# A two-layer diffusion backbone: more work of the expert layers put between the decoding of the keys and its transposes

## The chip, the core and the metric

The kernel runs on one core of one Trainium2 chip. The metric is the device time of one execution in microseconds (us). The engines are TensorE (PE, matmuls), VectorE (DVE), ScalarE (ACT), GpSimd (POOL) and SyncE (SP, which here only starts DMAs). Each engine works through its own queue of instructions in order and waits at semaphores for the others.

## The reference, cut to what matters

A sequence of 256 latent tokens and 256 context tokens, 1024 wide, passes two layers. Each layer is a token mixer (layer 1: mLSTM, layer 2: RWKV-7) and a retrieval of experts (PEER). Six modulation rows per layer come from a product of a conditioning vector with `ada_w`. All is float32. The retrieval is where the change lies:

```
# 8 heads, 2 x 128 product keys, 16 picks per head, 128 x 128 = 16384 experts
q        = h @ wq                         # per head two halves of 128
s1, s2   = top16(q1 @ keys1), top16(q2 @ keys2)
gate, (i, j) = top16 of the sums s1 + s2  # softmax over 16; expert number = 128*i + j
y[t]     = sum over the 8*16 picks of  gate * gelu(h[t] . u[128*i + j]) * v[128*i + j]
```

The kernel does not gather per token. It computes gelu(h . u) for all 128 x 128 experts, "row" j of 128 experts at a time, multiplies by a gate matrix that is zero where an expert wasn't picked, and sums with all rows of `v`. Only 128 of the tokens in layer 1 go by gathers (`urows`, `vtab`) of their picked experts.

## The kernel before, in words

**Products.** A float32 product is three matmuls in a rounded format: a weight block is loaded raw (512 KB), ACT writes its high half (`hi_w`, L77), DVE or GpSimd the remainder (`lo_w`, L78: raw minus high), and `mm3` (L97 to L99) issues high by high, high by low, low by high. A row of `u` takes 24 such matmuls. In layer 1 (`peer_two`) a row is 384 columns wide (256 of the context, 128 latent tokens), its two lo halves are 512 wide each and raw data lies in a ring of seven slots called `unit`; in layer 2 (`peer_one`) a row is 256 columns wide, its lo half is one instruction 1024 wide, and rows go in pairs with one Gelu each (L1788). Both have three buffers for hi and for lo.

**Retrieval.** `retrieval` (L1253) computes queries and scores, takes the top 16, and decodes the picked pairs on DVE: a long run of small integer operations (L1344 to L1359) and four times a one-hot compare (L1364, 128 x 2048), a multiply (L1366), two sums (L1368) and a reduction (L1369) into `sel`. Then it calls `between`, in which a layer puts products of other rows, and behind that transposes the decoded keys `sel` (L1380) and the gates (L1385) on PE into `iT`, `jT` and `gT`, from which the gate matrices are built (one-hot matrices `A` on ACT, L1647 and L1648, `B` on DVE, products `gp`, L1672).

**Layer 1 around the change.** Rows 0 to 7 come first, for the context's columns only. `between` adds rows 8 to 19 with lo halves on GpSimd. After the transposes `u_rest` computes rows 20 to 51 (long) and then the missing columns of rows 0 to 7 (short, 128 wide), into slots A and C; beside it the 128 gathers go (L1580 on GpSimd, their dot products L1588 on DVE, `rows1` from L1566 holds the expert numbers). Every fourth row also advances `fill`, one modulation pass (`ada_pass`, L131: 16 loads of 512 KB into buffers of its own, 32 matmuls of 32 x 512, four transposes). Then the gate stage begins.

**Layer 2 around the change.** Rows 0 to 7, retrieval with rows 8 to 19 in `between` (lo halves on GpSimd), then rows 20 to 63 (odd rows and those below 24 on GpSimd, the rest on DVE), then the gates.

**Order.** The program is written through a tile framework whose scheduler sets the order of the instructions in each engine's queue by its own estimates; the order of the code is only its input. PSUM has eight banks; in layer 1 `u` rows rotate through b6 and b0, scores and transposes through b7 and b1, the modulation pass has b2, and b3 to b5 are not in use yet.

Of the kernel before, what the change touches and what calls it, by code (L numbers as in the profile page):

```python
# [12 lines left out]
F32 = DT.float32  # L13
# [23 lines left out]
def mkpool(tc, name, bufs=1, space=None, side=None):  # L37
    kw = dict(name=name, bufs=bufs, reuse_waits="tile")
    if space is not None:
        kw["space"] = space  # L40
    if side is not None:
        kw["side"] = side
    return tc.tile_pool(**kw)
# [38 lines left out]
def load_raw(E, src, n=1024, pool=None, bufs=None):  # L82
    raw = (pool or E.W).tile([128, n], F32, name="raw", tag="raw", bufs=bufs or E.rawbufs)
    if len(src.shape) == 3:
        E.nc.sync.dma_start(raw.rearrange("p (a b) -> p a b", a=src.shape[1]), src)
    else:
        E.nc.sync.dma_start(raw, src)
    return raw


def stream(E, src, n=1024, eng=None):
    return split(E, load_raw(E, src, n), E.W, "w", E.partbufs, n, eng)
# [35 lines left out]
    nc.scalar.activation(E.sc[:, :, 0:2].rearrange("p k s -> p s k"), cr, AF.Silu)  # L128


def ada_pass(E, A, l, q, mods, pool, ps_pool, tag, bufs, own=0, halves=(0, 1)):  # L131


    nc = E.nc
    ada_w, ada_b, mods_dr, modsT = A["ada_w"][l], A["ada_b"][l], E.mods_dr[l], mods[q]
    ps = ps_pool.tile([128, 512], F32, name="ada_ps", tag=tag, bufs=bufs)
    bt = pool.tile([128, 512], F32, name="ada_bt", bufs=1)
    nc.gpsimd.memset(bt, 0.0)
    offs = [q * 2048 + half * 1024 + n * 512 for half in halves for n in range(2)]
    for g, o in enumerate(offs):  # L140
        nc.sync.dma_start(bt[32 * g:32 * g + 2, :], rows_bc(ada_b[o:o + 512], 2))
    fetch = lambda kt: [load_raw(E, ada_w[kt * 128:(kt + 1) * 128, offs[2 * x]:offs[2 * x] + 1024], 1024,
                                 pool if own else None, own) for x in range(len(halves))]
    raws = fetch(0)
    for kt in range(KT):
        if kt:
            yield

        for g in range(len(offs)):
            nc.tensor.matmul(ps[32 * g:32 * g + 32, :], E.sc[:, kt, :], raws[g // 2][:, g % 2 * 512:g % 2 * 512 + 512],  # L150
                             start=kt == 0, stop=kt == KT - 1, tile_position=(0, 32 * g))
        if kt < KT - 1:
            raws = fetch(kt + 1)
    rows = slice(0, 32 * len(offs))
    nc.vector.tensor_tensor(bt[rows], ps[rows], bt[rows], op=ALU.add)
    for g, o in enumerate(offs):
        if o // D in (2, 5):
            nc.sync.dma_start(mods_dr[:, o:o + 512], bt[32 * g:32 * g + 2, :])
    cols = [x for x, half in enumerate(halves) if 2 * q + half != 5]
    if cols:  # L160
        tp = ps_pool.tile([128, 4, 4, 32], F32, name="ada_tp", tag=tag, bufs=bufs)
        for blk in range(4):
            nc.tensor.transpose(tp[:, blk].rearrange("p g s -> p (g s)"), bt[:, blk * 128:(blk + 1) * 128], E.ident)
        for s in range(2):
            for x in cols:
                nc.vector.tensor_copy(modsT[:, s, halves[x]].rearrange("p (g b) -> p g b", g=2),
                                      tp[:, :, 2 * x:2 * x + 2, s].rearrange("p b g -> p g b"))
        m = {0: 1, 2: 0}.get(q)
        if m in halves:
            nc.vector.tensor_scalar(modsT[:, :, m, :], modsT[:, :, m, :], 1.0, None, op0=ALU.add)  # L170
    yield
# [7 lines left out]
def advance(gen, n):  # L179

    for _ in gen:
        if n is not None:
            n -= 1
            if n <= 0:
                break
# [1250 lines left out]
def peer_two(E, H0, h1, end, wq, keysT, uT, urows, vtab, filler):  # L1436
# [23 lines left out]
    with open_w(E, 2, 3), ExitStack() as pc:  # L1460
# [70 lines left out]
        def u_rows(j0, j1, t0=0, eng=None):  # L1531
            for j in range(j0, j1):
                up = ps_u.tile([128, TD], F32, name="u_ps")
                u_prod(up[:, t0:], halves(load(uT[j]), eng), t0)
                S.activation(row(j)[:, t0:], up[:, t0:], AF.Gelu)  # L1535
                yield


        with mkpool(tc, "route", 1) as R:
            for j in range(0, EARLY, 2):  # L1540
                up = (ps_u, ps_m)[j // 2 % 2].tile([128, 2, T], F32, name="u0_ps")
                for x in range(2):
                    u_prod(up[:, x], halves(load(uT[j + x])), 0, T, H0)
                S.activation(slots[0][:, j:j + 2, 0:T], up, AF.Gelu)
            for x in range(2):
                for y in range(2):
                    S.activation(H[x][:, 4 * y:4 * y + 4, 0:T], H0[x][:, 4 * y:4 * y + 4].bitcast(F32), AF.Copy)
            turn[:] = 0, NU
            H1 = [R.tile([128, KT, T], F32R, name=f"hr{x}") for x in range(2)]
            for x in range(2):  # L1550
                raw = R.tile([128, 4, T], F32, name="hraw", tag="eq", bufs=1)
                nc.sync.dma_start(raw.rearrange("p k t -> p (k t)"), h1[x])
                ks = slice(4 * x, 4 * x + 4)
                S.activation(H1[0][:, ks], raw, AF.Copy)
                V.tensor_tensor(H1[1][:, ks], raw, H1[0][:, ks].bitcast(F32), op=ALU.subtract)
                for y in range(2):
                    S.activation(H[y][:, ks, T:], H1[y][:, ks, 0:128].bitcast(F32), AF.Copy)
                xp = ps_m.tile([128, 4, 128], F32, name="x_ps")
                for k in range(4):
                    nc.tensor.transpose(xp[:, k, :], raw[:, k, 128:T], E.ident)  # L1560
                S.activation(xt[:, x * 512:(x + 1) * 512], xp.rearrange("p k d -> p (k d)"), AF.Copy)

            def between(picked):
                gate, sel = picked[1]
                V.tensor_copy(gate1, gate[:, 1].rearrange("p h c -> p (h c)"))
                V.scalar_tensor_tensor(rows1, sel[:, 1, 1].rearrange("p h c -> p (h c)"), 128.0,  # L1566
                                       sel[:, 0, 1].rearrange("p h c -> p (h c)"), op0=ALU.mult, op1=ALU.add)
                advance(u_rows(EARLY, EARLY + LATER, eng=G), None)

            Hs = [[[t[:, kt, 0:T] for kt in range(KT)] for t in X] for X in (H, H1)]  # L1570
            retrieval(E, R, ps_u, ps_m, Hs, [(*i, g[:, :, 0], g[:, :, 1]) for i, g in zip(idx, gT)], wq, keysT,
                      between, load)
# [27 lines left out]
        def interleave(*gens):  # L1600

            todo = [[0.0, 1.0 / n, g] for g, n in gens]
            while todo:
                todo.sort(key=lambda t: t[0])
                t = todo[0]
                t[0] += t[1]
                try:
                    next(t[2])
                except StopIteration:
                    todo.remove(t)  # L1610
# [3 lines left out]
        def fetch(n):  # L1614
            return itertools.islice(fs, n), n
# [3 lines left out]
                          i[0].rearrange("p (g x t) -> p g x t", x=2, t=8)[:, :, 0])  # L1619
        PC = pc.enter_context(mkpool(tc, "slotC", 1))  # L1620
        slots.append(PC.tile([128, NA - NX, TD], F32, name="slotC"))
        with mkpool(tc, "early", 1) as X:
            fill = filler(X, ps, "b2", 1)

            def u_rest():
                for x, _ in enumerate(itertools.chain(u_rows(EARLY + LATER, NA), u_rows(0, EARLY, T))):
                    if x % 4 == 0:
                        advance(fill, 1)
                    yield

            interleave((u_rest(), NA - LATER), fetch(GS[0]))
            advance(fill, None)
        bctx = pc.enter_context(ExitStack())
        PB = bctx.enter_context(mkpool(tc, "slotB", 1))
        slots.append(PB.tile([128, NB, TD], F32, name="slotB"))
# [114 lines left out]
def peer_one(E, end, H0, wq, keysT, uT, vtab):  # L1750
# [6 lines left out]
    JH = 64  # L1757
    JP = 96
    EARLY = 8
    LATER = 12  # L1760
    with open_w(E, 3, 3), ExitStack() as pc:
        misc = pc.enter_context(mkpool(tc, "pmisc", 1))
        oh = pc.enter_context(mkpool(tc, "poh", 2))
# [14 lines left out]
        def u_pair(j, gated, early=False):  # L1778
            ps = ps_u.tile([128, 2, T], F32, name="u_ps", tag="u")
            for x in range(2):  # L1780
                proj(E, ps[:, x, :], stream(E, uT[j + x], eng=G if early and (x or j < 24) else None), H)
            sl = slot(j, 2)
            if gated:
                a = misc.tile([128, 2, T], F32, name="act", bufs=2)
                S.activation(a, ps, AF.Gelu)
                V.tensor_tensor(sl, sl, a, op=ALU.mult)
            else:
                S.activation(sl, ps, AF.Gelu)  # L1788
# [135 lines left out]
def build(tc, A, out):  # L1924
    with ExitStack() as ctx:
# [32 lines left out]
        def end1(u, ep, ps, tag, acc, y1=None):  # L1958
            s = 1 - u
            if u == 0:  # L1960
# [3 lines left out]
                                  m1[0][:, s, 1, :], h_tile=hk[u], bufs=2, y1=y1)  # L1964

        peer_two(E, H0, h1, end1, A["wqT"][0], A["keysT"][0], A["uT"][0], A["urows"], A["vtab"][0],
                 lambda *p: ada_pass(E, A, 1, 0, m1, *p, own=2))
        H3 = []

        def epi2(acc, ps, tag):  # L1970
# [96 lines left out]
```

## Time and profile before

| | us |
|---|---|
| runs of the kernel before | 3315.76, 3321.59, 3330.23 (median 3321.59) |
| the profiled execution, on the device | 3324.07 |
| its span in the profile | 3322.2 |
| PE busy | 3062.8 (92%) |
| DVE busy | 2472.1 (74%) |
| ACT busy | 1543.7 (46%) |
| GpSimd busy | 743.5 (22%) |

The profiled execution's own time is 1.9 us above its span, and 2.5 us above the median of the runs. Busy times overlap, so they say little of what the end waits for. The rows further down are taken from views of the trace: a timeline row has the start and the duration of an instruction (or of several equal ones in a row, x4), its engine, line and operation, and in brackets how long the engine had stood idle before it and what ended that; a row of grouped lines has the count, the busy time and the mean in ns; a row of windows has the busy time of PE, PE's weight loads, DVE, ACT and GpSimd in a stretch of 20 us, the granted clock of PE as a share of full speed, the share of the DMA engines that was busy, and GB/s.

### The profile page before, as it was taken

The page shows a single profiled execution, that of the slowest core. Times are in us where ns is not written, and L with a number is a line of the kernel's source. Part 1 is how long each engine was busy: PE and PEld are TensorE (multiplying, and loading weights), DVE is VectorE, ACT ScalarE, POOL GpSimd, SP SyncE. Part 2 cuts the span into 40 slices and gives each one's busy share as a digit, 9 for nine tenths or more (in the row PEclk, how much of TensorE's full clock was granted, in tenths as well). Part 3 has the DMA queues.
Part 4 walks back from the last instruction along what each step waited for, and adds up shares of the span by engine and source line. Part 5 has one row for each costly group of instructions (what it writes and reads, how often), then busy time and mean ns, then how long its engine had stood idle before and what let it go on. Part 6 is the DMA issues. An engine that isn't in the chain of part 4 may idle for free.

```text
span 3322.2 us, 54675 instructions
## 1 busy us (share of the span) xinstructions
PE 3062.8 (92%) x20325; PEld 2627.3 (79%) x20325; DVE 2472.1 (74%) x5438; ACT 1543.7 (46%) x2867; POOL 743.5 (22%) x660
## 2 busy tenths in 40 slices
PE   7999999899999899999997887778889799999998
PEld 4776799799988789877875764477878799888887
DVE  5838679757978788899788638995767529887555
ACT  3524343335733333465444447466744343444443
POOL 1010044331033333303342310021307430000000
PEclk8999999898999999999998999889999899999999
DMA  5236532585368788836884257675744454556554
GB/s 211 88 98 201 198 137 70 211 301 200 120 224 272 246 275 285 291 130 241 288 280 141 91 167 214 190 203 161 230 150 147 139 185 153 170 172 223 191 190 146
DMA packets 251882, 633.82 MB, mean 191 GB/s; under 512 B 39840, under 2 KB 97312, under 8 KB 251360
## 3 DMA queue, kind: packets, MB, share of 16 engines
q1 hardware_dynamic: 180672, 478.27, 43.8%
q0 software_dynamic: 37152, 135.28, 12.1%
q10 hardware_dynamic: 33792, 16.78, 1.8%
q8 instruction: 159, 2.61, 0.3%
q14 instruction: 107, 0.88, 0.1%
HBM read 589.06 MB, written 41.19 MB: 190 GB/s over the span
## 4 chain that ended last, share of the span: by engine, by line
PE 68%; DVE 17%; DMA 6%; issue 5%; ACT 2%; POOL 2%; SPq 0%; ACTq 0%; DVEq 0%; POOLq 0%
PE acc L1714 11%; PE acc L1819 11%; PE u_ps L97 8%; PE u_ps L99 7%; PE u_ps L98 7%; DMA unit<-urows,rows 2%; PE gp L1672 2%; PE ada_ps L150 2%; DVE lo_w L78 1%; DMA raw<-ada_w 1%; PE vo L99 1%; DVE o_qk L326 1%; PE vo L98 1%; PE vo L97 1%; DVE xm L666 1%
## 5 line engine op out<-in xcount | busy, mean ns | idle before, releaser
L77 ACT ACTIVATE hi_w<-raw 128x1024 fp32r<-128x1024 f32 x339 | 358.2, 1057 | 528.6 <-PE u_ps L98 228.8
L78 DVE TENSOR_TENSOR lo_w<-raw,hi_w 128x1024 fp32r<-128x1024 f32 x287 | 354.1, 1234 | 320.6 <-ACT hi_w L77 320.4
L77 ACT ACTIVATE hi_w<-unit 128x512 fp32r<-128x512 f32 x522 | 326.4, 629 | 494.1 <-PE u_ps L98 279.7
L78 DVE TENSOR_TENSOR lo_w<-unit,hi_w 128x512 fp32r<-128x512 f32 x498 | 337.9, 687 | 152.1 <-ACT hi_w L77 150.1
L99 PE MATMUL u_ps<-hd,lo_w 128*128 128x384 f32 (+1 forms) x1024 | 348.7, 341 | 24.4 <-DVE lo_w L78 20.8
L97 PE MATMUL u_ps<-hd,hi_w 128*128 128x384 f32 (+1 forms) x1024 | 352.3, 344 | 4.1 <-ACT hi_w L77 3.0
L98 PE MATMUL u_ps<-hd,hi_w 128*128 128x384 f32 (+1 forms) x1024 | 347.8, 340 | 0.0
L97 PE MATMUL u_ps<-carry,hi_w 128*128 128x256 f32 x1088 | 310.2, 285 | 4.5 <-ACT carry L210 4.5
L99 PE MATMUL u_ps<-carry,lo_w 128*128 128x256 f32 x1088 | 308.4, 283 | 5.9 <-POOL lo_w L78 5.9
L98 PE MATMUL u_ps<-carry,hi_w 128*128 128x256 f32 x1088 | 307.9, 283 | 0.0
L1714 PE MATMUL acc<-hi_w,wh 128*128 128x512 f32 x718 | 282.9, 400 | 7.9 <-ACT hi_w L77 6.2
L1714 PE MATMUL acc<-lo_w,wh 128*128 128x512 f32 x718 | 283.9, 395 | 5.5 <-DVE lo_w L78 5.4
L1714 PE MATMUL acc<-hi_w,wl 128*128 128x512 f32 x718 | 282.6, 394 | 0.0
L1580 POOL DMA_INDIRECT unit<-urows,rows x128 | 165.9, 1296 | 428.7 <-DVE unit L1588 249.7
L1580 POOL DMA_INDIRECT unit<-vtab,rows x128 | 179.9, 1406 | 360.9 <-DVE xt L1593 171.0
L99 PEld LDWEIGHTS u_ps<-hd,lo_w 128*128 128x128 f32 x1024 | 198.6, 194 | 29.3 <-DVE lo_w L78 24.3
L99 PEld LDWEIGHTS u_ps<-carry,lo_w 128*128 128x128 f32 x1088 | 207.3, 191 | 6.7 <-POOL lo_w L78 6.7
L97 PEld LDWEIGHTS u_ps<-carry,hi_w 128*128 128x128 f32 x1088 | 207.9, 191 | 5.5 <-ACT carry L210 4.9
L97 PEld LDWEIGHTS u_ps<-hd,hi_w 128*128 128x128 f32 x1024 | 198.8, 194 | 12.7 <-ACT slotC L1535 5.9
L98 PEld LDWEIGHTS u_ps<-carry,hi_w 128*128 128x128 f32 x1088 | 207.6, 191 | 0.8 <-DVE carry L211 0.2
L98 PEld LDWEIGHTS u_ps<-hd,hi_w 128*128 128x128 f32 x1024 | 198.5, 194 | 1.2
L1588 DVE SCALAR_TENSOR_TENSOR unit<-unit,xt 128x1024 f32<-128x1024 f32 x128 | 155.3, 1219 | 41.4 <-DMA unit<-urows,rows 41.4
(523 smaller groups left out, 7493.9 us busy)
## 6 DMA issues: line engine op xcount, KB each, us to landing
raw<-vtab SPq DMA_DIRECT2D x144, 512.0 KB
unit<-uT SPq DMA_DIRECT2D x136, 512.0 KB
unit<-vtab SPq DMA_DIRECT2D x128, 512.0 KB
raw<-uT SPq DMA_DIRECT2D x128, 512.0 KB
raw<-ada_w SPq DMA_DIRECT2D x96, 512.0 KB
PK<-dr_pk SPq DMA_DIRECT2D x64, 448.0 KB
raw<-w_qkT SPq DMA_DIRECT2D x16, 512.0 KB
raw<-w_in SPq DMA_DIRECT2D x16, 512.0 KB
```

Of the source, the lines that this page charges most:

```text
L77: nc.scalar.activation(hi, raw, AF.Copy)
L78: (eng or nc.vector).tensor_tensor(lo, raw, hi.bitcast(F32), op=ALU.subtract)
L97: mm(out, lhi, rhi, start=start, stop=False)
L98: mm(out, lhi, rlo, start=False, stop=False)
L99: mm(out, llo, rhi, start=False, stop=stop)
L150: nc.tensor.matmul(ps[32 * g:32 * g + 32, :], E.sc[:, kt, :], raws[g // 2][:, g % 2 * 512:g % 2 * 512 + 512], start=kt == 0, stop=kt == KT ...
L326: V.scalar_tensor_tensor(dst, src, cw[:, ct, k:k + 1], dst, op0=ALU.mult, op1=ALU.add)
L1580: G.indirect_dma_start(out=t, out_offset=None, in_=src, in_offset=bass.IndirectOffsetOnAxis(ap=rows1[:, s:s + 1], axis=0))
L1588: return V.scalar_tensor_tensor(t, t, 1.0, xt, op0=ALU.mult, op1=ALU.mult, accum_out=act[:, s:s + 1])
L1672: mm(gp[:, t], At[t], Bg[:, x, t // 2, :, t % 2], start=x == 0, stop=x == 1)
L1714: mm(accs[2 * tt + n], l[:, ts], r, start=j == 0 and y == 0, stop=j == 127 and y == 2)
L1819: mm(acc[tt * 2 + n], l[:, x, ts], r[:, n * 512:(n + 1) * 512], start=(j + x == 0 and l is wh and r is vhi), stop=(j + x == 127 and l is wl))
```

## The change

In layer 1 the modulation pass leaves `u_rest` and is issued whole inside `between`, with raw data in the ring of `unit` slots and not in buffers of its own. After it the products of rows 20, 21 and 22 go to the banks b3 to b5, lo halves on GpSimd; their Gelus follow once slot C is open. `u_rest` then holds 29 long and 8 short rows and no modulation pass. In layer 2 `LATER` goes from 12 to 28, so that rows 8 to 35 stand in `between`, all of them with lo halves on GpSimd.

```
-def ada_pass(E, A, l, q, mods, pool, ps_pool, tag, bufs, own=0, halves=(0, 1)):
+def ada_pass(E, A, l, q, mods, pool, ps_pool, tag, bufs, own=0, halves=(0, 1), load=None):
...
-    fetch = lambda kt: [load_raw(E, ada_w[kt * 128:(kt + 1) * 128, offs[2 * x]:offs[2 * x] + 1024], 1024,
-                                 pool if own else None, own) for x in range(len(halves))]
+    load = load or (lambda src: load_raw(E, src, 1024, pool if own else None, own))
+    fetch = lambda kt: [load(ada_w[kt * 128:(kt + 1) * 128, offs[2 * x]:offs[2 * x] + 1024])
+                        for x in range(len(halves))]
...
+            beside = []
+
             def between(picked):
...
                 advance(u_rows(EARLY, EARLY + LATER, eng=G), None)
+                advance(filler(R, ps, "b2", 1, load=load), None)
+
+                for x in range(3):
+                    beside.append((EARLY + LATER + x, ps.tile([128, TD], F32, name="u_ps", tag=f"b{3 + x}", bufs=1)))
+                    u_prod(beside[x][1], halves(load(uT[beside[x][0]]), G))
...
-        with mkpool(tc, "early", 1) as X:
-            fill = filler(X, ps, "b2", 1)
-
-            def u_rest():
-                for x, _ in enumerate(itertools.chain(u_rows(EARLY + LATER, NA), u_rows(0, EARLY, T))):
-                    if x % 4 == 0:
-                        advance(fill, 1)
-                    yield
-
-            interleave((u_rest(), NA - LATER), fetch(GS[0]))
-            advance(fill, None)
+        for j, up in beside:
+            S.activation(row(j), up, AF.Gelu)
+        u_rest = itertools.chain(u_rows(EARLY + LATER + len(beside), NA), u_rows(0, EARLY, T))
+        interleave((u_rest, NA - LATER - len(beside)), fetch(GS[0]))
...
 def peer_one
-    LATER = 12
+    LATER = 28
...
-                proj(E, ps[:, x, :], stream(E, uT[j + x], eng=G if early and (x or j < 24) else None), H)
+                proj(E, ps[:, x, :], stream(E, uT[j + x], eng=G if early and (x or j < EARLY + LATER) else None), H)
...
-                 lambda *p: ada_pass(E, A, 1, 0, m1, *p, own=2))
+                 lambda *p, **k: ada_pass(E, A, 1, 0, m1, *p, **k))
```

The lines of the changed kernel have numbers one higher than before from L139 on, and eight higher behind `between` of layer 1.

What the scheduler makes of it on PE in layer 1, at the transposes of the decoded keys. In the kernel before, the matmuls of row 20 (`u_ps`) go on between the transposes (`tp`), the first three of them ahead of the transposes of the gates:

```order
L99 MATMUL u_ps<-hd_3189,lo_w 128x384
L1380 MATMUL tp<-ident,sel 128x128 x4
L97 MATMUL u_ps<-hd_3189,hi_w 128x384
L98 MATMUL u_ps<-hd_3190,hi_w 128x384
L99 MATMUL u_ps<-hd_3189,lo_w 128x384
L1385 MATMUL tp<-ident,gate 128x128 x2
L97 MATMUL u_ps<-hd_3189,hi_w 128x384
L1380 MATMUL tp<-ident,sel 128x128
```

In the changed kernel the same place on PE reads (`ada_ps` is the modulation pass):

```order
L99 MATMUL u_ps<-hd_3189,lo_w 128x384
L151 MATMUL ada_ps<-unit,sc_lhs 32x512 x14
L1381 MATMUL tp<-ident,sel 128x128 x4
L151 MATMUL ada_ps<-unit,sc_lhs 32x512 x2
L1386 MATMUL tp<-ident,gate 128x128 x2
L1381 MATMUL tp<-ident,sel 128x128 x2
L1386 MATMUL tp<-ident,gate 128x128
L151 MATMUL ada_ps<-unit,sc_lhs 32x512 x4
L1673 LDWEIGHTS A
L1673 MATMUL gp<-Bg,A 128x52
```

The last two rows are the first of 16 such pairs (the first gate products); two ada matmuls, 16 more pairs, ten ada matmuls and the four transposes of the modulation pass follow, and only then the first matmul of row 20. So 14 of the 32 ada matmuls moved ahead of the transposes, and rows 20 to 22 did not.

On ACT in the changed kernel the same place has two complete builds of `A` ahead of all but one of the high halves of rows 20 to 22:

```order
L77 ACTIVATE hi_w<-unit 128x512
L1536 ACTIVATE slotA<-u_ps 128x384 x2
L1648 ACTIVATE A<-iota_65,iF_3182 128x128 x8
L1649 ACTIVATE A<-A 128x1024
L1648 ACTIVATE A<-iota_65,iF_3182 128x128 x8
L1649 ACTIVATE A<-A 128x1024
L77 ACTIVATE hi_w<-unit 128x512 x5
L1631 ACTIVATE slotC<-u_ps 128x384
```

Before, there was one build at this place, with high halves between its parts.

In layer 2, on PE, the place of the transposes in the kernel before:

```order
L98 MATMUL u_ps<-carry_24518,hi_w 128x256
L99 MATMUL u_ps<-carry_24517,lo_w 128x256
L1380 MATMUL tp<-ident,sel 128x128 x4
L97 MATMUL u_ps<-carry_24517,hi_w 128x256
L98 MATMUL u_ps<-carry_24518,hi_w 128x256
L99 MATMUL u_ps<-carry_24517,lo_w 128x256
L1385 MATMUL tp<-ident,gate 128x128 x2
```

The changed kernel has the same rows around its transposes, with 384 more matmuls (16 rows) ahead of them. On GpSimd the last run of lo halves goes from

```order
L1298 TENSOR_TENSOR cand<-sv 128x2x16
L78 TENSOR_TENSOR lo_w<-raw,hi_w 128x1024 x32
```

before to this in the changed kernel:

```order
L1299 TENSOR_TENSOR cand<-sv 128x2x16
L78 TENSOR_TENSOR lo_w<-raw,hi_w 128x1024 x38
```

The six more are the even rows 24 to 34, which DVE made before.

## Rows read from the trace of the kernel before

**Rows 1.** The page, the chain that ended last: its engines.

```profile
PE 68%; DVE 17%; DMA 6%; issue 5%; ACT 2%; POOL 2%; SPq 0%; ACTq 0%; DVEq 0%; POOLq 0%
```

**Rows 2.** Timeline of PE, layer 1, at the transposes.

```profile
594.59 0.34 PE L99 MATMUL u_ps<-hd,lo_w 128*128 128x384 f32 x1
594.77 0.60 PE L1380 MATMUL tp<-ident,sel 128*128 128x128 f32 x4
...
610.02 0.69 PE L99 MATMUL u_ps<-hd,lo_w 128*128 128x384 f32 x1 [14.30 <-DVE lo_w L78]
...
613.28 0.67 PE L97 MATMUL u_ps<-hd,hi_w 128*128 128x384 f32 x1
...
618.23 0.40 PE L98 MATMUL u_ps<-hd,hi_w 128*128 128x384 f32 x1
```

**Rows 3.** Timeline of PE, layer 1, the first ada group.

```profile
622.72 1.05 PE L150 MATMUL ada_ps<-raw,sc_lhs 128*32 128x512 f32 x4
623.70 0.45 PE L99 MATMUL u_ps<-hd,lo_w 128*128 128x384 f32 x1
```

**Rows 4.** Timeline of PE, layer 2, at the transposes.

```profile
2588.77 0.28 PE L99 MATMUL u_ps<-carry,lo_w 128*128 128x256 f32 x1
2600.20 0.69 PE L1380 MATMUL tp<-ident,sel 128*128 128x128 f32 x2 [11.14 <-DVE sel L1369]
2609.05 0.69 PE L1380 MATMUL tp<-ident,sel 128*128 128x128 f32 x2 [8.17 <-DVE sel L1369]
```

**Rows 5.** Windows of 20 us: the one in layer 1's short rows.

```profile
770.00:790.00 20.00, 18.78 (x105) 18.50 (x103) 12.17 (x21) 5.86 (x13) 4.28 (x3) 0.63 0.79 284
```

**Rows 6.** Timeline of ACT, layer 2, Gelus of the pairs (20, 21) and (62, 63).

```profile
2619.05 0.58 ACT L1788 ACTIVATE slotA<-u_ps 128x512 f32<-128x512 f32 x1
...
2738.33 0.58 ACT L1788 ACTIVATE slotA<-u_ps 128x512 f32<-128x512 f32 x1
```

**Rows 7.** Timeline of GpSimd, layer 2, lo halves beside the decoding and behind it.

```profile
2566.74 14.67 POOL L78 TENSOR_TENSOR lo_w<-raw,hi_w 128x1024 fp32r<-128x1024 f32 x6 [2.75 <-ACT hi_w L77]
...
2587.32 5.32 POOL L78 TENSOR_TENSOR lo_w<-raw,hi_w 128x1024 fp32r<-128x1024 f32 x2 [0.34 <-ACT hi_w L77]
2616.29 2.39 POOL L78 TENSOR_TENSOR lo_w<-raw,hi_w 128x1024 fp32r<-128x1024 f32 x1 [23.65 <-ACT hi_w L77]
```

**Rows 8.** Lines of DVE, layer 2, 2566.7 to 2592.7, while GpSimd works.

```profile
L1364 DVE TENSOR_TENSOR eq<-partH,iota 128x2048 f16<-128x2048 f16 x1 | 3.5, 3450 | 0.0
L1357 DVE TENSOR_SCALAR part<-fi 128x256 uint32<-128x256 uint32 x1 | 2.5, 2462 | 0.0
L1355 DVE TENSOR_SCALAR part<-fi 128x256 uint32<-128x256 uint32 x1 | 0.3, 293 | 0.0
```

**Rows 9.** Lines of DVE, layer 2, 2593.7 to 2609.1, GpSimd idle.

```profile
L1368 DVE TENSOR_TENSOR eq<-eq 128x1024 f16<-128x1024 f16 (+1 forms) x8 | 4.5, 558 | 0.2
L1364 DVE TENSOR_TENSOR eq<-partH,iota 128x2048 f16<-128x2048 f16 x3 | 3.7, 1226 | 0.1
```

**Rows 10.** Timeline of DVE, layer 1, the end of the decoding.

```profile
610.48 0.69 DVE L78 TENSOR_TENSOR lo_w<-unit,hi_w 128x512 fp32r<-128x512 f32 x1
...
612.26 0.29 DVE L1566 SCALAR_TENSOR_TENSOR rows<-sel 128x128 int32<-128x128 f32 x1
```

**Rows 11.** Timeline of ACT, layer 1, the short rows and the next build of `A`.

```profile
773.95 0.63 ACT L77 ACTIVATE hi_w<-unit 128x512 fp32r<-128x512 f32 x1 [3.67 <-DMA unit<-uT]
...
776.29 0.26 ACT L1535 ACTIVATE slotA<-u_ps 128x128 f32<-128x128 f32 x1
...
790.92 0.26 ACT L1535 ACTIVATE slotA<-u_ps 128x128 f32<-128x128 f32 x1
791.32 2.52 ACT L1647 ACTIVATE A<-iota,iF 128x128 f16<-128x128 f16 x8
...
795.54 1.04 ACT L1648 ACTIVATE A<-A 128x1024 f16<-128x1024 f16 x1
```

**Rows 12.** Waits of SyncE's queue, 540 to 640: us in total, times, longest.

```profile
SPq L87 <- PE ada_ps L150: 8.9, 3, 4.8
```

## The prediction, made before the changed kernel was run

> **What bounds the kernel now.** I read the chain of waits first [rows 1]: two thirds of the span are TensorE (PE), so a change pays where PE stands still, and the busy shares of other engines are worth nothing by themselves. Then PE's timeline at the two places where the decoded keys are transposed.
>
> Layer 1: after row 19 PE runs four transposes at 594.77 and then stands until 610.02; it needs the lo half of row 20, which VectorE (DVE) makes behind the decoding. Row 20 itself gets going at 613.28, at half clock until 618.23 [rows 2]. A full-clock step of a 384-column matmul is 594.77 - 594.59 = 0.18 us [rows 2] (0.174 over many), so a row of 24 is 4.2 us. The 41 row matmuls before the first ada group at 622.72 [rows 3] would take 41 x 0.174 = 7.1 us at full clock: the stream stands as if it had started at 615.6.
>
> Layer 2: rows 8 to 19 end at 2588.77; PE waits 11.14 and 8.17 us for the decoded `sel`, on either side of two transposes [rows 4]. Then rows 20 to 63 flow: two Gelus 21 pairs apart, 2619.05 and 2738.33, give 5.68 a pair, 2.84 a row [rows 6]. DVE is what both places wait for.
>
> **Layer 2, LATER 12 to 28.** Sixteen rows (20 to 35), 384 matmuls, move from behind the transposes to ahead of them; none are added. Of their lo halves six move from DVE to GpSimd (even rows 24 to 34), the other ten were on GpSimd already. If nothing slowed the decoding, PE would go on from 2588.9 and the 44 rows would end at 2588.9 + 44 x 2.84 + 1.2 for the transposes = 2715, a gain of 23 us. That is the upper bound.
>
> But the decoding does slow. While GpSimd ran its ten lo halves from 2566.7 to 2592.64 [rows 7], the one-hot compare L1364 took 3450 ns [rows 8]; afterwards a compare took 1226 ns and a sum L1368 558 [rows 9], and I price the multiply as the compare. GpSimd's 2.39 us a lo, alone, against 2.66 in the pair that met a large compare and a multiply [rows 7], says that the two engines take turns: one lo, one DVE operation. At 2592.64 GpSimd is done with row 21, and the decoding has some 15.4 us of undisturbed work left, from 2593.7 to 2609.05 [rows 4]. With the change 14 more lo halves (22 to 35) lie beside it: 14 x 2.39 = 33.5 us, plus the DVE operations let in between, three compares and three multiplies at 1.23, eight sums at 0.56, a small one: about 12 us. So lo 35 is ready at 2592.64 + 45.5 = 2638.1, the decoding ends near 2640, and row 35 on PE at 2638.1 + 2.84 = 2640.9: both limits fall together. With 1.2 us of transposes row 36 starts near 2642; 28 rows x 2.84 = 79.5 give 2721.5 against 2738.3: a gain of 17 us. PE would wait some 0.4 us a row on the way, in short pieces; I take its clock as full.
>
> The Trainium skill bears on this: "SBUF — State Buffer", section Who interferes with whom, says that DVE and GpSimd share one pair of ports as an exclusive lock, that a tensor_tensor with both inputs in SBUF contends, and that whoever starts first blocks the other for its whole instruction. The trace agrees (3450 against 1226 ns). By that rule the change is hurt, since every extra lo may block the decoding; by taking turns the sum stays as above, by always losing it becomes the second rival.
>
> **Layer 1.** What is put beside the decoding is a modulation pass (32 ada matmuls, 16 loads) and three rows. The order on PE says how much of it truly lies there: 14 ada matmuls stand ahead of the four `sel` transposes, then everything else behind them: 18 ada matmuls, 32 gate matmuls, four ada transposes, and only then row 20. PE executes its queue in order, so the three rows are not beside the decoding at all.
>
> The decoding is rid of two DVE lo halves of 0.69 each that sat among its sums (the second at 610.48) [rows 10], so it ends 1.3 us before 612.26, at 610.9. The 14 ada matmuls run before that in PE's idle time and cost nothing. What then stands ahead of row 20 is a chain: transposes and casts until 612.0 (they led to ACT's first A build 1.1 us after the decoded rows before); ACT's two A builds, now ahead of row 20's hi half, 2.52 + 1.04 us each [rows 11], so 615.6 and 619.1; sixteen gate matmuls after each, which I estimate at 2 us a set (1 to 4); ten ada matmuls at 0.25 (four took 0.98 before the next row matmul [rows 3]) to 0.5 at half clock, ending between 623.6 and 626; then the bias and four transposes, 1 us or less. I take 626.5 for row 20, with 618 (only the second gate set counts) and 650 as ends. Against the 615.6 of before that is 10.9 us late.
>
> In return the ada matmuls leave the row stream. A group of four delays the next row matmul by 0.98 + 0.1 [rows 3]; eight groups and four transposes come to 9.6 us. So the long rows end 10.9 - 9.6 = 1.3 us later; their length by itself is unchanged, three of them only having a bank of their own.
>
> Behind them eight short rows end at 790.92. The clock fell there to 0.63 of full [rows 5] after ACT waited 3.67 us for a `uT` load, and the last three rows took 790.92 - 776.29 = 14.6 us [rows 11]; at the full clock they would take about half. Nothing in the change touches this tail except that loads come in another phase: I take 0, with -7 (no fall of the clock) and +12 (the fall from its first row) as ends. The gate tiles that DVE now builds early were needed later anyway: 0, with -3 as the other end.
>
> **Sum** against the profiled execution: 3324.07 - 17 + 1 + 0 = 3308; this execution stands 2.5 us above the median of the runs (3321.59), so 3305 or 3306 on their basis. I say 3305.
>
> **Rivals.**
> A second way down: in layer 1 the moved work costs nothing and the tail keeps its clock. For it: the fall comes after a single 3.67 us wait, which another phase of loads could miss. Against: the order, with row 20 behind the gates. It gives -8 (row 20 at 618) or -7 (the tail), so about 3297.
>
> Second, the lock starves the decoding in layer 2. For it: a DVE operation of 0.29 us takes 2.46 while GpSimd works [rows 8], and six lo halves ran 2.445 each, hardly hindered [rows 7]. Against: one DVE operation got in per lo even so. If the decoding stood until the last lo (about 2634, at PE's pace) and then needed its 15.4 us, row 36 starts at 2651 and PE idles long enough to restart at half clock, 2.5 us as from 613.28 to 618.23 [rows 2]: a gain of 17 - 9 - 2.5 = 5, so 3316 to 3318.
>
> Third, slower: in layer 1 the nine ada loads left behind the transposes go one by one through the ring of seven slots, which now alternate with gathers that wait for `rows1`. For it: SyncE has waited for ada matmuls up to 4.8 us at a time [rows 12]. Against: 14 ada matmuls are done by about 600, so most slots are free and filled again long before 611. Five such waits of 4.8 us would start row 20 at 650, 24 us later than I take; with layer 2's 17 that gives 3305 + 24 = 3329. It decides from a start of row 20 at 643 on.
>
> Fourth, that the change doesn't do what it says (three rows beside the decoding) is not a rival here but part of the forecast: it is why layer 1 is priced at 1 and not at three rows of 4.2 us less.
>
> **How the numbers follow.** Forecast 0.62, the second way down 0.15, starved decoding 0.16, slower 0.07. What a measurement of this kernel can tell from no change is 0.5%, 16.6 us: below 3305.0 counts as faster, above 3338.2 as slower. The forecast lies on the first bound, so half of it falls to either side: faster 0.62 x 0.48 + 0.15 x 0.95 = 0.44; slower: half of the third rival and a little of the rest, 0.05; the rest 0.51. The forecast's own range is 3298 to 3313; to 8 in 10 it reaches into both neighbours, 3293 to 3321.
>
> **What would show it.** In layer 2: the four `sel` transposes near 2640 less any shift, with next to no wait ahead of them; compares and multiplies near 3 us in this stretch; the last pair's Gelu 17 us nearer to the stage's start. In layer 1: 14 ada matmuls right behind 595, PE idle to 611, row 20 near 626, long rows ending within 3 us of before. The prediction is wrong if row 20 starts at 618 or 640, if the decoding in layer 2 ends after 2645, or if the tail of short rows moves by over 5 us.

## The result, and the profile after

The changed kernel takes 3302.55 us (median of five runs, 3297.34 to 3303.71); the kernel before, with two more runs beside it, 3326.39 (3315.76 to 3330.23). The ratio on record is 0.9941, 95% interval 0.9923 to 0.9960: some 20 us (13 to 26) faster. (The ratios here are those on record; they are not quotients of the medians, which in this case lie 23.8 us apart.) The forecast was 3305, 16.6 us below the median known then. The profiled execution of the changed kernel took 3297.34 us with a span of 3295.5.

Layer 2 first, at the place of [rows 4]. Timeline of PE after the change, the end of row 35 and the transposes:

```profile
2627.09 0.28 PE L99 MATMUL u_ps<-carry,lo_w 128*128 128x256 f32 x1
2627.21 0.38 PE L1381 MATMUL tp<-ident,sel 128*128 128x128 f32 x2
2629.19 0.44 PE L1381 MATMUL tp<-ident,sel 128*128 128x128 f32 x2 [1.60 <-DVE sel L1370]
```

Of the 19.3 us that PE waited there before, 1.6 are left. What GpSimd did in the meantime, the rows that answer to [rows 7]; the first (rows 21 and 22) is the last with a counterpart there, then come 14 more lo halves (rows 23 to 35, and 37, since DVE makes row 36's):

```profile
2580.20 5.31 POOL L78 TENSOR_TENSOR lo_w<-raw,hi_w 128x1024 fp32r<-128x1024 f32 x2 [0.43 <-ACT hi_w L77]
2585.88 8.34 POOL L78 TENSOR_TENSOR lo_w<-raw,hi_w 128x1024 fp32r<-128x1024 f32 x3 [0.37 <-ACT hi_w L77]
2594.67 29.41 POOL L78 TENSOR_TENSOR lo_w<-raw,hi_w 128x1024 fp32r<-128x1024 f32 x10 [0.46 <-ACT hi_w L77]
2625.64 2.50 POOL L78 TENSOR_TENSOR lo_w<-raw,hi_w 128x1024 fp32r<-128x1024 f32 x1 [1.55 <-ACT hi_w L77]
```

Which rows these are follows from ACT in the kernel before, which writes a high half as soon as PE leaves the row three places ahead, since there are three buffers:

```profile
2586.18 1.06 ACT L77 ACTIVATE hi_w<-raw 128x1024 fp32r<-128x1024 f32 x1 [1.20 <-PE u_ps L98]
2589.02 1.06 ACT L77 ACTIVATE hi_w<-raw 128x1024 fp32r<-128x1024 f32 x1 [1.78 <-PE u_ps L98]
2615.16 1.06 ACT L77 ACTIVATE hi_w<-raw 128x1024 fp32r<-128x1024 f32 x1 [24.59 <-PE u_ps L98]
```

PE's last matmul of row 19 starts at 2588.77, so the high half of 2589.02 is row 22's, and GpSimd's lo half behind it, the last before its long pause in [rows 7], is row 22's too. Row 23's follows only when row 20 has left PE.

And DVE's groups in the same stretch (2585 to 2629; columns as in [rows 9]):

```profile
L1369 DVE TENSOR_TENSOR eq<-eq 128x1024 f16<-128x1024 f16 (+1 forms) x8 | 19.2, 2396 | 0.2
L1367 DVE TENSOR_TENSOR eq<-eq,sv 128x2048 f16<-128x2048 f16 x4 | 13.4, 3338 | 0.1
L1365 DVE TENSOR_TENSOR eq<-partH,iota 128x2048 f16<-128x2048 f16 x3 | 7.8, 2590 | 0.1
L1370 DVE TENSOR_REDUCE sel<-eq 128x128 f32<-128x512 f16 x4 | 2.7, 687 | 0.1
```

A sum that took 558 ns beside an idle GpSimd takes 2396 here, a compare 2590 instead of 1226; only the reduction keeps its 0.69. Fifteen operations of the first three groups stand beside 14 lo halves, about one for one: the two engines do take turns. That the reductions go through is what the same section of the Trainium skill ("SBUF — State Buffer", Who interferes with whom) says of them, and these rows agree.

Layer 1, at the place of [rows 2]. Timeline of PE after the change:

```profile
590.63 3.63 PE L151 MATMUL ada_ps<-unit,sc_lhs 128*32 128x512 f32 x28
594.19 0.66 PE L1381 MATMUL tp<-ident,sel 128*128 128x128 f32 x4
595.48 1.05 PE L151 MATMUL ada_ps<-unit,sc_lhs 128*32 128x512 f32 x4 [0.63 <-DMA unit<-ada_w]
609.72 0.69 PE L1386 MATMUL tp<-ident,gate 128*128 128x128 f32 x2 [13.19 <-DVE iT L1383]
...
616.29 2.77 PE L151 MATMUL ada_ps<-unit,sc_lhs 128*32 128x512 f32 x20
619.85 0.66 PE L164 MATMUL ada_tp<-ident,ada_bt 128*128 128x128 f32 x4 [0.80 <-DVE ada_bt L156]
620.26 0.42 PE L97 MATMUL u_ps<-hd,hi_w 128*128 128x384 f32 x1
...
622.95 0.45 PE L99 MATMUL u_ps<-hd,lo_w 128*128 128x384 f32 x1 [2.08 <-POOL lo_w L78]
```

(The profile counts each ada matmul of the order twice.) PE still stands 13.19 us beside the decoding, and row 20 comes after the whole pass. Ahead of it ACT and GpSimd do this:

```profile
615.07 2.56 ACT L1648 ACTIVATE A<-iota,iF 128x128 f16<-128x128 f16 x8 [1.30 <-PE gp L1673]
617.66 1.06 ACT L1649 ACTIVATE A<-A 128x1024 f16<-128x1024 f16 x1
618.85 1.15 ACT L77 ACTIVATE hi_w<-unit 128x512 fp32r<-128x512 f32 x2
```

```profile
620.64 0.95 POOL L1588 DMA_INDIRECT unit<-urows,rows  x1 [0.30 <-PE ada_tp L164]
621.62 2.51 POOL L78 TENSOR_TENSOR lo_w<-unit,hi_w 128x512 fp32r<-128x512 f32 x2
```

The lo half that PE waits for at 622.95 stands behind a gather in GpSimd's queue. The end of the row stage is that of ACT in [rows 11], now:

```profile
756.41 0.48 ACT L1536 ACTIVATE slotC<-u_ps 128x384 f32<-128x384 f32 x1
...
772.07 0.63 ACT L77 ACTIVATE hi_w<-unit 128x512 fp32r<-128x512 f32 x1 [3.20 <-DMA unit<-uT]
...
783.19 0.26 ACT L1536 ACTIVATE slotA<-u_ps 128x128 f32<-128x128 f32 x1
```

with a granted clock of 0.74 from 770 to 790 (before 0.63). To compare stages of different executions I measure them from a common point. In layer 1 that is the first score matmul, in layer 2 the last one; both are on one row of the line's view, here of the changed kernel, with the Gelus (first and last start):

```profile
L1285 PE MATMUL sc_ps<-keys,qT x192: 270/275/377, 432.1 to 2542.7; 128*128 128x128 f32 x192
...
L1789 ACT ACTIVATE slotB<-u_ps x16: 571/577/585, 2718.0 to 2820.9; 128x512 f32<-128x512 f32 x16
```

So layer 2's row stage, last score to first Gelu of slot B, is 2718.0 - 2542.7 = 175.3 us. In the kernel before it was 2745.1 - 2549.8 = 195.3: 20.0 us shorter. The same for ten kernels of this study, one profiled execution each, in us (those of e5 and e6 are given with them):

| kernel | L1: last long Gelu | L1: last short Gelu | L1: first Gelu of slot B | clock 770 to 790 | L2: row stage |
|---|---|---|---|---|---|
| before | 325.7 | 356.2 | 363.4 | 0.63 | 195.3 |
| changed | 324.3 | 351.1 | 356.6 | 0.74 | 175.3 |
| e1 layer 2 only | 325.7 | 348.6 | 353.2 | 1.00 | 174.8 |
| e2 layer 1 only | 327.9 | 355.0 | 361.0 | 0.86 | 194.3 |
| e3 rows first | 316.5 | 343.2 | 348.8 | 0.77 | 175.3 |
| e4 pass only | 323.5 | 356.4 | 361.8 | 0.55 | 176.5 |
| e7 rows only | 325.2 | 365.0 | 371.2 | 0.50 | 175.3 |
| e9 rows only, late gather | 317.7 | 356.8 | 363.0 | 0.50 | 175.3 |
| e8 rows first, mixed | | | 342.0 | 1.00 | 176.7 |
| e10 before, mixed | | | 355.9 | 1.00 | 193.9 |

### The profile page after: what moved, and what is told of

The parts are those of the page before. It is cut to its first block, busy times and chain, and to the rows that moved or that the text cites. A ratio compares the mean times of both kernels' runs of the same rounds, so it can differ in the third digit from the quotient of the medians.

```text
span 3295.5 us, 54703 instructions
## 1 busy us (share of the span) xinstructions
PE 3053.1 (93%) x20325; PEld 2616.2 (79%) x20325; DVE 2495.4 (76%) x5426; ACT 1542.7 (47%) x2867; POOL 766.9 (23%) x672
## 4 chain that ended last, share of the span: by engine, by line
PE 68%; DVE 17%; DMA 7%; issue 5%; ACT 2%; POOL 2%; SPq 0%; ACTq 0%; DVEq 0%; POOLq 0%
PE acc L1715 12%; PE acc L1820 11%; PE u_ps L97 7%; PE u_ps L99 7%; PE u_ps L98 7%; PE gp L1673 2%; PE ada_ps L151 2%; DMA unit<-urows,rows 1%; DVE lo_w L78 1%; DVE o_qk L327 1%; DMA raw<-ada_w 1%; DVE eq L1369 1%; DMA unit<-uT 1%; DVE xm L667 1%; PE vo L99 1%
## 5 line engine op out<-in xcount | busy, mean ns | idle before, releaser
L77 ACT ACTIVATE hi_w<-raw 128x1024 fp32r<-128x1024 f32 x339 | 358.1, 1057 | 504.4 <-PE u_ps L98 208.6
L78 DVE TENSOR_TENSOR lo_w<-raw,hi_w 128x1024 fp32r<-128x1024 f32 x281 | 345.8, 1231 | 277.2 <-ACT hi_w L77 277.1
L97 PE MATMUL u_ps<-hd,hi_w 128*128 128x384 f32 (+1 forms) x1024 | 348.3, 340 | 2.1 <-ACT hi_w L77 1.0
L98 PE MATMUL u_ps<-hd,hi_w 128*128 128x384 f32 (+1 forms) x1024 | 344.3, 336 | 0.0
```

Of the source, the lines that this page charges most:

```text
L77: nc.scalar.activation(hi, raw, AF.Copy)
L78: (eng or nc.vector).tensor_tensor(lo, raw, hi.bitcast(F32), op=ALU.subtract)
L97: mm(out, lhi, rhi, start=start, stop=False)
L98: mm(out, lhi, rlo, start=False, stop=False)
```

## The experiments

From the two profiles I took theory A: layer 2 brings some 20 us of the gain and layer 1 the rest, 4 to 7. The rivals: layer 1 brings half, or, as the prediction has it, nothing, because the three rows stay behind the transposes, and the 5 us seen at the end of its row stage are chance.

**e1, layer 2's part alone**

```
# kernel before, in peer_one
-    LATER = 12
+    LATER = 28
-    ... eng=G if early and (x or j < 24) else None
+    ... eng=G if early and (x or j < EARLY + LATER) else None
```

Expected: 

> Layer 2's part alone (28 rows beside the decoding), layer 1 as before. Theory A, layer 2 brings 20 of the 24 us: 20 us below the kernel before, and from the last score matmul to the first acc matmul of layer 2 about 20 us less than before, as in the changed kernel (298 before, 278 changed). Rival, layer 1 brings half: 12 us below.

Measured: 3299.1 us against 3317.61, ratio 0.9940 (0.9920 to 0.9960), the ratio of the whole change. The row stage of layer 2 is 174.8 us. Layer 1, whose code is that of before, ended 10 us earlier than in the profile of before: its last long Gelu comes at the same 325.7, but the short rows took 22.9 us instead of 30.5, and the clock stayed at 1.00. In stretches of 5 us the granted clock of the kernel before is at or near 0.5 for some 20 us from 775 on; half of that, as an estimate the time lost by it, is about the 10.2 us by which the two executions differ at slot B (363.4 and 353.2).

**e2, layer 1's part alone**

```
# changed kernel, in peer_one
-    LATER = 28
+    LATER = 12
-    ... (x or j < EARLY + LATER)
+    ... (x or j < 24)
```

Expected: 

> Layer 1's part alone, layer 2 as before. Theory A: 4 to 7 us below the kernel before, from the end of the long rows (1 us) and from the tail of short rows and the start of the gate stage (5 us). Rival, the 5 us of the tail are the chance of one execution (phase of the loads and the clock): within 2 us of before. By the prediction: 1 us above.

Measured: 3321.55 us against 3317.61, ratio 1.0004 (0.9989 to 1.0018). The 4 to 7 us that I had read from one profile don't stand; the rival and the prediction (1 us above) hold. In five profiled executions of the changed layer 1 (the changed kernel, e2, and e5, e6_later20 and e6_later36 below) the first Gelu of slot B comes 356.6 to 361.0 us after the first score, with a mean of 358.1; in two of the layer 1 of before 353.2 and 363.4, mean 358.3.

**e3, the three rows ahead of the modulation pass**

```
# changed kernel, in between()
-                advance(filler(R, ps, "b2", 1, load=load), None)
                 for x in range(3):
                     ...
+                advance(filler(R, ps, "b2", 1, load=load), None)
```

Expected: 

> The changed kernel with the three rows ahead of the modulation pass in the code, so that 72 row matmuls stand ahead of the transposes on PE as the change says. Theory A: PE has 12.5 us of rows in an idle time of 14; six lo halves on GpSimd hold up the decoding by about 0.5 us each and are held up by it, so the decoding ends 3 us later: 9 us below the changed kernel. Rival, the lock: each of the six lets one DVE operation wait 1.3 us or more, the decoding ends 8 us later or more: within 4 us of the changed kernel.

Measured: 3291.02 us against 3317.61, ratio 0.9908 (0.9884 to 0.9932); the long rows end at 316.5, 7.8 us earlier than in the changed kernel. Its timeline of PE:

```profile
604.69 3.63 PE L151 MATMUL ada_ps<-unit,sc_lhs 128*32 128x512 f32 x28
608.25 0.66 PE L1381 MATMUL tp<-ident,sel 128*128 128x128 f32 x4
610.02 1.05 PE L151 MATMUL ada_ps<-unit,sc_lhs 128*32 128x512 f32 x4 [1.12 <-DMA unit<-ada_w]
616.82 0.69 PE L1386 MATMUL tp<-ident,gate 128*128 128x128 f32 x2 [5.74 <-DVE iT L1383]
```

The pass starts 14 us later than in the changed kernel (1.5 of them the execution's own shift), since three rows lie ahead of it, and PE's longest wait falls from 13.19 to 5.74. The six lo halves cost the decoding some 5.6 us: measured from the first score, its transposes' wait ends 5.6 us later (616.82 - 433.6 against 609.72 - 432.1), between the two forecasts. So the three rows were worth 8 us, and the change as made didn't collect them.

**e7, the rows without the pass**

```
# changed kernel: between() without the pass; u_rest as in the kernel before, with 29 long rows
-                advance(filler(R, ps, "b2", 1, load=load), None)
...
+            fill = filler(X, ps, "b2", 1, own=2)
...
+                    if x % 4 == 0:
+                        advance(fill, 1)
```

Expected: 

> The changed kernel without the moved modulation pass: it is back in the row stream with its own buffers, the three rows alone stand in between. Theory A, that the pass costs 9.6 us in the stream and that moving it costs as much in front of row 20: 9 us below the changed kernel, like the kernel with rows first, since rows start right at the transposes again. Rival, moving the pass is worth its 9.6 us when rows come first: 5 us or more above the kernel with rows first.

Measured: 3313.34 us, ratio 0.9983 (0.9967 to 0.9999): 14 us worse than the changed kernel, a miss. The rival's number (5 us or more above e3) came out, but the cause that the rows show first belongs to neither theory. PE's one wait in the stretch, from its timeline, and GpSimd's rows there:

```profile
613.39 0.69 PE L99 MATMUL u_ps<-hd,lo_w 128*128 128x384 f32 x1 [16.40 <-POOL lo_w L78]
```

```profile
610.82 1.21 POOL L1586 DMA_INDIRECT unit<-urows,rows  x1 [18.24 <-DVE rows L1569]
612.06 1.27 POOL L78 TENSOR_TENSOR lo_w<-unit,hi_w 128x512 fp32r<-128x512 f32 x1
```

The lo half that PE waits for stands in GpSimd's queue behind a gather that needs `rows1`, the last thing that is decoded. All transposes are behind these rows on PE, so the keys come late as well: the first at 624.1, where the decoding had ended by 610.8. On top of it the short rows ran at a clock of 0.50.

**e9, the rows without the pass, gathers later**

```
# e7
-            interleave((u_rest(), NA - LATER - len(beside)), fetch(GS[0]))
+            ur = u_rest()
+            advance(ur, 6)
+            interleave((ur, NA - LATER - len(beside) - 6), fetch(GS[0]))
```

Expected: 

> The kernel with the rows alone beside the decoding, and the first gathers asked for six rows later in the code, so that all lo halves of rows 20 to 22 stand ahead of the first gather in GpSimd's queue. Theory: in the kernel with the rows alone, PE waited 16.4 us because the last lo halves stood behind a gather that needs the decoded rows; without that, the three rows run beside the decoding and the long rows end 8 us earlier, near 317 us after the first score matmul (325 there, 316.5 with rows first). Rival, what stops the rows is another thing that the modulation pass in the stream brings, the buffers that its loads wait for: PE stands at row 21 or 22 again and the long rows end at 323 or later.

Measured: the long rows end at 317.7, as the theory said: the gather in the queue was the cause in e7. The time is 3301.7 us, ratio 0.9944 (0.9924 to 0.9964), no better than e1: the short rows took 39.1 us, some 30 of them at half the clock, so the 8 us were given back at the end of the stage.

**e4, the pass without the rows**

```
# changed kernel, in between(): the loop over x in range(3) is left out, u_rest starts at row 20
```

Expected: 

> The changed kernel without the three rows in spare banks; they are in the row stream again. Theory: in the changed kernel these rows stand behind the modulation pass and all its waits, so it makes no difference where their banks are: the long rows end within 2 us of the changed kernel (324.3 us after the first score matmul) or of layer 1's part alone (327.9). Rival, their bank or the late Gelu is worth something: 4 us later or more.

Measured: one run, 3306.32 us; long rows end at 323.5, within 1 us of the changed kernel. The spare banks bring nothing where the rows stand in the changed kernel.

**e8, rows first and the short rows mixed in**

```
# e3
-        u_rest = itertools.chain(u_rows(EARLY + LATER + len(beside), NA), u_rows(0, EARLY, T))
+        def u_rest():
+            short = u_rows(0, EARLY, T)
+            for x, _ in enumerate(u_rows(EARLY + LATER + len(beside), NA)):
+                yield
+                if x % 3 == 2 and next(short, 0) is None:
+                    yield
```

Expected: 

> The kernel with rows first, and in addition the eight short rows not at the end of the stage but one behind every third long row. The theory: the end of layer 1's row stage varies between 23 and 40 us in the five traces so far because eight short rows need 512 KB each in 2.7 us of products, ACT waits for these loads, and PE's clock falls after it. Mixed in, the loads are asked for evenly and no row waits: 8 x 2.7 = 22 us for them, 5 us below the kernel with rows first, with a granted clock of 1.00 throughout the row stage. Rival: the loads as a whole are the bound, and the same waits come elsewhere: within 2 us of the kernel with rows first.

Measured: 3284.9 us against 3322.11, ratio 0.9884 (0.9858 to 0.9909), the fastest kernel of the study; the first Gelu of slot B comes at 342.0, 6.8 us earlier than in e3. Windows of 40 us around the start of slot B, which comes at 773.6 (columns as in [rows 5]):

```profile
750.00:770.00 20.00, 20.00 (x117) 20.00 (x116) 12.43 (x20) 8.23 (x15) 4.08 (x3) 1.00 0.90 306
770.00:790.00 20.00, 20.00 (x207) 19.27 (x206) 15.17 (x36) 13.27 (x31) 0.00 (x0) 1.00 0.40 132
```

and, for the contrast, one window of e9, in its short rows, where PE is as busy at half the clock:

```profile
770.00:790.00 20.00, 20.00 (x106) 20.00 (x106) 10.79 (x18) 5.51 (x12) 2.61 (x3) 0.50 0.85 301
```

PE's clock is at its upper level of 2.4 GHz in the one and at its lower, 1.2 GHz, in the other. ACT still waits for `uT` loads in e8 (11.7 us in all, 2.3 at most), but PE has a long row to work on then.

**e10, the kernel before with the short rows mixed in**

```
# kernel before, in u_rest: a short row behind every third long row, the pass every fourth row as before
```

Expected: 

> The kernel before, with one edit: the short rows of layer 1 one behind every third long row and not at the end. Theory: from the last row's end to the gate stage nothing waits for loads, PE's clock stays at 1.00, and the row stage ends as with the best tail seen, 348 to 350 us after the first score matmul for the first Gelu of slot B (363.4 in the profile of before, 353.2 in the kernel with layer 2's part alone): 5 to 10 us below before, and runs that differ by less. Rival, with the modulation pass in the stream the loads are the bound as a whole: within 3 us of before.

Measured: 3317.08 us against 3318.89, ratio 0.9996 (0.9983 to 1.0009): no gain, a miss. In the profile the clock is 1.00 from 770 to 790 and slot B starts at 355.9. ACT waits 13.7 us for `uT` loads (10.3 in the kernel before), now among the long rows, but the rival's reason, that loads are the bound, doesn't hold either: from 190 us behind the first score to slot B PE is hardly ever idle, in e10 (first row) as in e1, where the short rows come last (columns as in [rows 5]):

```profile
622.00:788.00 166.00, 164.12 (x1040) 154.29 (x1039) 104.76 (x177) 65.86 (x128) 56.92 (x39) 0.99 0.87 309
622.00:785.00 163.00, 162.13 (x1037) 153.14 (x1035) 104.40 (x175) 65.58 (x127) 56.11 (x39) 1.00 0.88 314
```

PE's own work fills the stage, so mixing gives back only what an execution loses to the clock: 10 us in the profile of before, nothing in e1. How much the other runs of before lose isn't known; it was too little to show. The 6.8 us of e8 over e3 fit this: e3 spent some 10 us of this stretch at the lower level, half of it lost, and idled 2.7 us, e8 none and 1.5. Mixing in the changed kernel without the rows first was not run.

**e5, the extra even rows' lo halves on DVE**

```
# changed kernel, in peer_one
-    ... eng=G if early and (x or j < EARLY + LATER) else None
+    ... eng=G if early and (x or j < 24) else None
```

Expected: 

> The changed kernel with the even rows 24 to 34 of layer 2 on VectorE again (LATER stays 28). Theory A: GpSimd is needed because VectorE's queue holds these lo halves behind the decoding: PE stands at row 24 until the decoding ends, and the row stage of layer 2 is 10 to 14 us longer than in the changed kernel. Rival, the port between the two engines is what holds the decoding up, and eight lo halves there instead of 14 let it end 10 us earlier: as fast as the changed kernel or 2 us faster.

Measured: 3313.54 us, ratio 0.9973 (0.9954 to 0.9992); layer 2's row stage 189.1 us, 13.8 longer than in the changed kernel, as theory A had it. PE's waits there:

```profile
PE u_ps L99 <- DVE lo_w L78: 13.7, 1, 13.7
```

Row 24 stands until the decoding is over. The rival had one thing right: with fewer lo halves beside it the decoding ends 63.3 us after the last score matmul, not 86.4. But though lo halves on GpSimd slow the decoding, DVE makes them too late.

**e6, LATER 20 and LATER 36**

```
# changed kernel, in peer_one
-    LATER = 28
+    LATER = 20      # and 36
```

Expected of 20: 

> The changed kernel with LATER 20 in layer 2, eight rows fewer beside the decoding. Theory A: each lo half on GpSimd costs the decoding about 1.9 us; with six instead of 14 ahead it ends near 2589 + 14 us at 2610 in the time base of the changed kernel, PE is done with row 27 at 2604 and waits about 6 us; with the restart at the lower clock the stage is 8 us longer than with 28. Rival, the lo halves do not hold up the decoding in sum: it ends by 2604 and the stage is as long as with 28.

Expected of 36: 

> The changed kernel with LATER 36 in layer 2, eight more rows beside the decoding. Theory A: with 28 PE waits 1.6 us for the last reduction, so more rows can bring 2 us at most. Rival, GpSimd starves the decoding for as long as there are lo halves: the transposes come 22 us later but behind rows that would be done anyway, and the gate stage starts later because its tables do: 2 to 6 us longer than with 28.

Measured, one run each: with 20, 3308.37 us, row stage 184.5 us, 9.2 longer than with 28. PE's wait with 20:

```profile
PE tp L1381 <- DVE sel L1370: 9.0, 1, 9.0
```

With 36, 3291.6 us, row stage 175.4 us, the same as with 28, and PE waits for lo halves only, 1.4 us in all. From the last score matmul to the end of the last reduction the decoding takes 59.2, 71.1, 86.4 and 85.4 us with LATER 12, 20, 28 and 36: beside it stand six lo halves more with 20 than with 12 (rows 23 to 27 and 29) and eight more again with 28, which cost it 12 and 15 us, 1.9 to 2.0 us each; with 36 it meets no more than with 28, since it ends before they come. With 28 both ends meet; more rows are free but gain nothing.

## Why the prediction was right

- **Layer 2, a gain of 17 us.** Right in its mechanism, 3 us too small: 20.0 us in the profiles, 0.9940 for this part alone. The two limits do fall together: row 35 leaves PE at 2627.2, the decoding ends at 2629.1. The term that was mis-sized is the sum over GpSimd, 33.5 + 12 = 45.5 us, by its count and by its price. At 2592.64 GpSimd was done with row 22 and not 21, so 13 lo halves stood ahead of row 36 and not 14. And I had added the whole length of each DVE operation, 0.86 us a lo: from the end of lo 22 (2585.51) to the end of lo 35 (2624.08) it is 38.6 us, with 0.8 of waits for ACT, or 2.90 a lo, 0.51 above its 2.39 alone: GpSimd did not wait for the whole of a DVE operation each time. Each lo half was ready when PE came to its row (row 35's by 0.3 us), and PE's own pace, 2.84 a row, was the limit up to there, without the 0.4 us a row that I gave it. Row 36 started 5.5 us earlier than forecast when the execution's shift of 7.1 us is taken off; 2.3 us of that went again, because I had priced the last 28 rows by their matmuls alone, without the transposes of the gates and the first wait for a lo half (1.2) and without the way from the last matmul to the Gelu (1.1).
- **Layer 1 worth nothing.** Right in the order that it rests on: PE's queue has the rows behind the pass. That the size fits so well is in part luck. Row 20 starts at 620.26, its first lo matmul at 622.95: as a stream at full clock it starts at 622.6, which is 625.2 in the time of before (its first score is 2.6 us later). I had taken 626.5. By the chain alone it was 3.6 us early: the two gate sets took 0.9 and 0.7 us of PE and not 2 each, and the second began at 615.64, before ACT's second build ended at 618.72, so it did not wait for that build as my chain has it. The wait for the lo half behind a gather, which my sum doesn't have, gave 2.3 us back. The long rows end 1.4 us earlier in the changed kernel and 2.2 later in e2, around the 1.3 later of the forecast. By itself the part measures 1.0004.
- **The tail at 0, between -7 and +12.** Right as a range and as a statement of ignorance. One code gave 30.5 and 22.9 us, another 26.8 and 27.1, and e7 and e9 39.8 and 39.1. The second way down (a full clock in the tail) happened, but in e1, with the layer 1 of before.
- **The rivals.** The starved decoding falls: with 36 rows ahead the decoding isn't any longer than with 28. The slow ring of slots falls: PE waited for `ada_w` loads 0.63 us. Row 20 was far from the 643 at which the third rival would have decided.
- **Not seen.** I took the order as a fact of the scheduler. That the two pieces in `between` need only be swapped for 8 us, and that with the short rows mixed in the clock was at 1.00 at the stage's end (in e8 and e10, but also in e1 without it), came from the experiments.

## What to carry to other kernels

Before pricing work as "beside" a long stretch of another engine, read in the queue's order what stands ahead of it: in an in-order queue one instruction that needs the stretch's result (a gather, a transpose) stops everything behind it. Where two engines hold each other up, count how many of their operations meet rather than their busy time, see which row each of them serves (with three buffers a helper is up to three rows ahead), and add rows until the two ends meet. Short, load-heavy rows between long ones kept the clock up here in both kernels that had them, and paid in one of them. Judge a stage that ends in a clock drop by several executions, since one profile of it can be off by 10 us.

## What the runs showed of the hardware that was not expected

The reduction on DVE kept its time beside GpSimd (687 against 688 ns) while a sum of the same tile rose from 558 to 2396. GpSimd lost much less by the turns (2874 ns in the mean of the 14, against 2390). And right behind a short pause of PE the granted clock went to its lower level at the end of layer 1. In e3 the pause is this row of PE's timeline:

```profile
767.02 0.33 PE L97 MATMUL u_ps<-hd,hi_w 128*128 128x128 f32 x1 [1.12 <-ACT slotA L1536]
```

In stretches of 5 us the clock is 0.90, 0.50, 0.58 and 1.00 from 765 on. In e9 a pause of 3.83 us was followed by some 30 us at half, in e7 one of 1.19 by some 34, in the kernel before one of 1.09 by some 20, with PE busy almost throughout; in e1 a pause of 0.87 us was followed by none. How long the lower level lasts doesn't go with the length of the pause in these executions, and what decides it stays open.
